# Hymba encoder layer on one core: the output projection by Strassen's seven products, all local heads in the second token chunk, low weight parts kept in DRAM

## The chip, the core and the metric

The kernel runs on one core of a Trainium2 chip. The metric is the device time of one execution in microseconds; lower is better. TensorE (PE in the profile, PEld for its weight loads), VectorE (DVE), ScalarE (ACT) and GpSimd (POOL) compute; SyncE (SP) issues every DMA of this kernel, in the order of its own instruction stream.

## The reference

One encoder layer, applied to a prompt of 1024 tokens and to a sample of 256 tokens, each with 16 meta tokens ahead. All in float32.

```python
def encoder_layer(h, ...):                           # h: tokens x 2048
    u = rms_norm(h, norm_w) @ w_in                   # 2048 x 6656: qa ka va za qb kb vb zb
    qa, ka = axial rope of per-head rms_norm(qa), rms_norm(ka)      # 8 query heads, 2 key heads
    ya = global_gqa(qa, ka, va) * silu(za)           # full attention, 8 heads of 128
    qb, kb = per-head rms_norm(qb), rms_norm(kb)     # 8 heads of 128
    yb = neighbourhood_attention(qb, kb, vb, rpb) * silu(zb)        # 8 x 16 window on a grid 64 wide
    return h + concatenate([ya, yb]) @ w_out         # 2048 x 2048; meta tokens are dropped at the end
```

## The kernel before

Every matrix of the layer is cut in strips of 128 output features, and everything is kept transposed (features on the partitions, tokens along the free axis). A float32 product is done in three matmuls on a rounded high part and a low part: high x high, high x low, low x high. `split` makes the two parts: ScalarE rounds the high part (L54), VectorE subtracts it from the full value (L55). So every tile of weights (`wr`, 128 x 512, 256 KB) costs one DMA, one ScalarE and one VectorE instruction, and gives `wh` and `wl`.

The 1296 token rows don't fit at once. **Chunk 1** (L431) has the meta tokens, the sample and 384 prompt tokens, **chunk 2** (L539) the other 640 prompt tokens. Each loads its x, splits it (L85, L86), and runs the 52 strips of the input projection (`strips`, L108: per strip 4 weight tiles, and 16 x 2 x 3 matmuls, L128 to L130). Both chunks read and split all the weights. Chunk 1 also does the sample's attention. Chunk 2 does the prompt's: 8 global heads of 4 blocks (`attend`, L243), with strips between them, and then the local heads (`attend_strip`, L338), 4 blocks each. Strips of the last four local heads (`NL = 4`) are done ahead, two after each global head (`FILL_A`), their results put in DRAM (`k2d`, `q2d`, `vn`, `zd`); their attention (`late_blocks`) is left for the output projection.

An attention block is a chain: score matmuls (L254 to L256, or L359 to L361), a maximum over partitions on GpSimd (L202), subtraction and exponential, a sum over partitions on GpSimd (L219), the matmuls with v (L294 to L296, or L393), and `put_y`, which scales, multiplies by z, splits the result into two parts and stores both in DRAM (`yd`).

The **output projection** (`outproj`, L758) is done in two halves of the 2048 inputs, eight heads each: the first half's y (`yh`, both parts, 1280 tokens, 1.25 MB a head) is loaded, 16 strips of 72 matmuls run (blocks of 512, 512 and 256 tokens), the sum with x goes to DRAM (`pd`), and the 16 blocks of the last four local heads are put between the first 12 strips. The second half does the same with the other heads and adds `pd`.

The order on each engine is made by a scheduler that works on a simulated timeline of the program, by priority and by what is ready; `high_priority(offset=woff)` moves weight loads and splits ahead. An engine, and SP, executes its stream in order. Buffers per tile name are the pools' `bufs` (4 for `raw`, 4 for `w`, 1 for `q`, `k`, `v`, `z`).

Of the kernel before, what the change touches and what calls it, by code (L numbers as in the profile page):

```python
# [37 lines left out]
NL = 4  # L38
FILL_A = 2
FILL_B = 1  # L40
LSTR = 12
YORD = (0, 4, 1, 5, 2, 6, 3, 7)
WCH = 4
OBL = [(0, 512), (512, 512), (1024, 256)]
# [3 lines left out]
class Kern:  # L48
# [59 lines left out]
    def strips(self, jobs, getx):  # L108

        nc, tc = self.nc, self.tc  # L110
        out = [[pool.tile([P, 512], F32, tag=tag, name="pp") for pool, tag in pools] for _, _, pools in jobs]
        for c in range(KT // WCH):
            ws = []
            for src, _, _ in jobs:
                with tc.high_priority(offset=self.woff):
                    w = self.raw.tile([P, WCH, P], F32, tag="raw", name="wr")
                    self.lastw = nc.sync.dma_start(w[:], src[:, c * WCH:(c + 1) * WCH, :]).ins
# [104 lines left out]
    def put_y(self, po, tot, zs, ydst):  # L222
# [7 lines left out]
        y = self.t.tile([P, QB], F32, tag="t", name="y")  # L230
# [6 lines left out]
        yt = self.y.tile([P, 2, QB], F32R, tag="y", name="yt")  # L237
        self.split(yt[:, 0, :], yt[:, 1, :], y[:])
        for i, d in enumerate(ydst):
            yi = yt[:, i, :].bitcast(F32)  # L240
            nc.sync.dma_start(d, yi.rearrange("p (g r) -> p g r", g=4) if len(d.shape) == 3 else yi)
# [183 lines left out]
    def project(self, *parts):  # L425

        jobs = [(self.io["w_in"][p[0]], p[1], [p[3] if len(p) > 3 else (self.pp, "pp")] * len(p[1])) for p in parts]
        out = self.strips(jobs, self.get_x)
        return [p[2](ps) for p, ps in zip(parts, out)]

    def chunk1(self):  # L431
        nc, io = self.nc, self.io
        self.woff = 0
# [68 lines left out]
        def run(h, q, z, k, v, vm, tab):  # L502
            k, km = k
            ydst = [self.yd[h][:, i, NP:] for i in range(2)]
# [34 lines left out]
    def chunk2(self):  # L539
        nc, io = self.nc, self.io  # L540
        self.start_chunk(io["x2"], T2)
# [119 lines left out]
        def run_block(h, b, q, z, k, v, tab):  # L661
            k, km = k
            v, vm = v
            if tab is not None:
                c = slice(64 * b, 64 * b + 64)
                self.attend_strip(q, strips_of(z[:])[:, :, c], k, km, v[b], vm[:], tab, b,
                                  [strips_of(self.yd[h][:, i, :NP])[:, :, c] for i in range(2)])
# [3 lines left out]
            self.attend(q[:, :, c], z[:, c], keys, km, v, vm[:], [self.yd[h][:, i, c] for i in range(2)])  # L671
# [5 lines left out]
        def late_blocks():  # L677
            for h in range(NH - NL, NH):
# [9 lines left out]
        for h in range(NH - NL, NH):  # L688
# [3 lines left out]
        late = late[:-2] + [late[-2:]]  # L692

        def fill(n):
            for _ in range(min(n, len(late))):
                p = late.pop(0)
                pr(*(p if isinstance(p, list) else [p]))

        for g in range(2):
# [5 lines left out]
            for h in range(4 * g, 4 * g + 4):  # L705
# [3 lines left out]
                fill(FILL_A)  # L709
        for h in range(NH - NL):  # L710
            for what in "kqvz":
                if what == "z":
                    z, = pr(z_strip(ZB + h, 8 + h))
                elif what == "v":
                    pr(v_local(VB + h, h))
                    v = v_windows(h)
                elif what == "q":
                    q, = pr(q_strip(QB_ + h, 8 + h, qwb, False))
                else:
                    k, = pr(k_strip(KB + h, 2 + h, kwb, False))  # L720
            run(8 + h, q, z, k, v, self.bias_table(h))
            fill(FILL_B if h < NH - NL - 1 else len(late))
        self.late_blocks = late_blocks()


    def load_y(self, pool, heads):
        nc = self.nc
        for h in heads:
            y = pool.tile([P, 2, NP + NS], F32R, tag=f"y{h}", name="yh")
            nc.sync.dma_start(y[:].bitcast(F32), self.yd[h][:])  # L730
            self.ys[h] = y[:, 0, :], y[:, 1, :]

    def out_strip(self, c, half, third):

        nc, tc = self.nc, self.tc
        ps = [self.pp.tile([P, 512], F32, tag="pp", name="pp") for _ in range(2)]
        ps.append(third[0].tile([P, 512], F32, tag=third[1], name="pp"))
        ws = []
        for i in range(2 * half, 2 * half + 2):
            with tc.high_priority(offset=self.woff):  # L740
                w = self.raw.tile([P, WCH, P], F32, tag="raw", name="wr")
                self.lastw = nc.sync.dma_start(w[:], self.io["w_out"][c][:, i * WCH:(i + 1) * WCH, :]).ins
                wh = self.w.tile([P, WCH, P], F32R, tag="wh", name="wh")
                wl = self.w.tile([P, WCH, P], F32R, tag="wl", name="wl")
                self.split(wh[:], wl[:], w[:])
                ws += [(wh[:, k, :], wl[:, k, :]) for k in range(WCH)]
        order = range(8) if half else YORD
        for blocks in (OBL[:2], OBL[2:]):
            for i, k in enumerate(order):
                wh, wl = ws[k]  # L750
                yh, yl = self.ys[8 * half + k]
                for o, n in blocks:
                    p = ps[o // 512]
                    nc.tensor.matmul(p[:, :n], wh, yh[:, o:o + n], start=i == 0, stop=False)  # L754
                    nc.tensor.matmul(p[:, :n], wh, yl[:, o:o + n], start=False, stop=False)  # L755
                    nc.tensor.matmul(p[:, :n], wl, yh[:, o:o + n], start=False, stop=i == 7)  # L756
        return ps

    def outproj(self, es_attn):

        nc, io = self.nc, self.io
        NT = NP + NS
        self.ys = {}
        self.load_y(self.ya, YORD)
        done = 0
        for c in range(16):
            while done < 4 * NL and done * LSTR < 4 * NL * (c + 1):
# [134 lines left out]
```

## Time and profile before

| | |
|---|---|
| three runs | 2297.64, 2296.99, 2293.76 us; median 2296.99 |
| the profiled execution | 2295.91 us, span 2294.1 us, granted clock 0.999 |
| instructions | 40464 |
| busy | PE 2268.6, PEld 2192.9, DVE 1601.9, ACT 1104.6, POOL 530.9 us |
| DMA | 290.17 MB, mean 126 GB/s |

A matmul row's duration counts from its start to the end of its results; the next matmul starts long before that end. So "busy" says whether PE had something running, and the cost of a matmul is the distance from its start to the next one's start. DVE and ACT rows overlap a little in the same way. DMA share is that of 16 engines.

### The profile page before, as it was taken

Reading aid. Unit: us, or ns where it says so; the run is one execution under the profiler, and the core shown is the slowest. Engines: PE = TensorE matmul, PEld = TensorE weight load, DVE = VectorE, ACT = ScalarE, POOL = GpSimd, SP = SyncE. Lnnn points to the kernel's source line nnn. Section 1 sums busy time; section 2 is a strip of 40 time slices with the busy share of each in tenths; the row PEclk is TensorE's granted clock in tenths of the full one; section 3 lists DMA queues with packets and bytes.
Section 4 is the critical chain, followed back from the end, with each engine's and each line's share of the span. In section 5 each row is a group of like instructions: output and inputs, shape, how many; then the busy total and the mean of one; then the engine's idle time right before and its main releaser. Section 6 shows DMA issues by size and latency. Waiting matters only on the chain.

```text
span 2294.1 us, 40464 instructions
## 1 busy us (share of the span) xinstructions
PE 2268.6 (99%) x15166; PEld 2192.9 (96%) x15166; DVE 1601.9 (70%) x3092; ACT 1104.6 (48%) x2400; POOL 530.9 (23%) x275
## 2 busy tenths in 40 slices
PE   7999999999999999999999999999999999999999
PEld 7999999999999999999999999999999888888888
DVE  6876775555555689999998989998777666652221
ACT  6654554444444566676666665665454333320000
POOL 0322232211121124223223314223233222210000
PEclk9999999999999999999999999999999999999999
DMA  6433333333333442222222222224444966657342
GB/s 199 137 111 112 110 105 111 107 106 106 102 108 107 134 153 72 90 86 75 91 93 87 88 81 75 87 84 138 116 133 115 336 214 191 191 182 277 133 136 79
DMA packets 205733, 290.17 MB, mean 126 GB/s; under 512 B 55360, under 2 KB 125408, under 8 KB 203488
## 3 DMA queue, kind: packets, MB, share of 16 engines
q1 hardware_dynamic: 205536, 287.58, 39.5%
q8 instruction: 119, 1.95, 0.4%
q14 instruction: 78, 0.64, 0.1%
HBM read 216.30 MB, written 64.63 MB: 122 GB/s over the span
## 4 chain that ended last, share of the span: by engine, by line
PE 54%; DVE 3%; ACT 1%; POOL 1%; issue 1%; DMA 1%; SPq 0%; DVEq 0%; POOLq 0%
PE pp L130 8%; PE pp L129 8%; PE pp L128 8%; PE pp L754 7%; PE pp L755 7%; PE pp L756 7%; PE po L393 2%; PE po L296 1%; PE po L294 1%; PE po L295 1%; PE sp L254 1%; PE sp L255 1%; PE sp L256 1%; POOL m L138 1%; PE sp L361 1%
## 5 line engine op out<-in xcount | busy, mean ns | idle before, releaser
L128 PE MATMUL pp<-xh,wh 128*128 128x384 f32 (+2 forms) x3328 | 1025.2, 311 | 11.8 <-ACT xh L85 11.6
L129 PE MATMUL pp<-xl,wh 128*128 128x384 f32 (+2 forms) x3328 | 1030.7, 310 | 1.1 <-DVE xl L86 0.8
L130 PE MATMUL pp<-xh,wl 128*128 128x384 f32 (+2 forms) x3328 | 1029.8, 311 | 0.0
L128 PEld LDWEIGHTS pp<-xh,wh 128*128 128x128 f32 x3328 | 624.1, 188 | 13.7 <-ACT xh L85 13.1
L129 PEld LDWEIGHTS pp<-xl,wh 128*128 128x128 f32 x3328 | 625.8, 188 | 3.4 <-DVE xl L86 3.3
L130 PEld LDWEIGHTS pp<-xh,wl 128*128 128x128 f32 x3328 | 625.7, 188 | 0.2
L55 DVE TENSOR_TENSOR wl<-wr,wh 128x512 fp32r<-128x512 f32 x480 | 368.7, 771 | 226.1 <-ACT wh L54 220.8
L54 ACT CAST wh<-wr 128x512 fp32r<-128x512 f32 x480 | 294.7, 617 | 416.2 <-PE pp L129 198.3
L138 POOL PARTITION_ALL_REDUCE m<-ms x104 | 246.4, 2369 | 423.2 <-ACT ms L136 299.9
L754 PE MATMUL pp<-yh,wh 128*128 128x512 f32 (+1 forms) x768 | 274.6, 358 | 2.5 <-DMA yh<-yd 2.5
L755 PE MATMUL pp<-yh,wh 128*128 128x512 f32 (+1 forms) x768 | 275.0, 358 | 0.0
L219 POOL PARTITION_ALL_REDUCE tot<-a x80 | 170.3, 2128 | 450.6 <-DVE a L217 450.5
L756 PE MATMUL pp<-yh,wl 128*128 128x512 f32 (+1 forms) x768 | 274.2, 358 | 0.0
L202 POOL PARTITION_ALL_REDUCE ma<-m x80 | 106.9, 1336 | 583.9 <-DVE m L200 570.2
L754 PEld LDWEIGHTS pp<-yh,wh 128*128 128x128 f32 x768 | 145.7, 190 | 24.0 <-DMA yh<-yd 2.6
L755 PEld LDWEIGHTS pp<-yh,wh 128*128 128x128 f32 x768 | 145.7, 190 | 20.9
L756 PEld LDWEIGHTS pp<-yh,wl 128*128 128x128 f32 x768 | 145.5, 190 | 20.8
L785 DVE TENSOR_TENSOR o<-pp,o 128x512 f32<-128x512 f32 (+1 forms) x48 | 28.5, 602 | 140.3 <-PE pp L756 140.3
L258 ACT COPY S<-sp 128x512 f32<-128x512 f32 x136 | 77.7, 581 | 61.1 <-PE sp L256 37.1
L275 ACT ACTIVATE S<-S 128x512 f32<-128x512 f32 x136 | 84.4, 629 | 30.1 <-DVE S L274 30.0
L61 ACT ACTIVATE rs_l<-m 128x384 f32<-128x384 f32 (+2 forms) x104 | 49.1, 472 | 102.4 <-DVE m L139 102.2
L55 DVE TENSOR_TENSOR pl<-S,ph 128x512 fp32r<-128x512 f32 x136 | 96.0, 719 | 0.0
(186 smaller groups left out, 3235.6 us busy)
## 6 DMA issues: line engine op xcount, KB each, us to landing
wr<-in_w_in SPq DMA_DIRECT2D x416, 256.0 KB, 3.2
yd<-yt SPq DMA_DIRECT2D x160, 128.0 KB, 2.4
yh<-yd SPq DMA_DIRECT2D x16, 1280.0 KB, 17.4
wr<-in_w_out SPq DMA_DIRECT2D x64, 256.0 KB, 4.0
pd<-o SPq DMA_DIRECT2D x16, 640.0 KB, 4.3
o<-pd SPq DMA_DIRECT2D x16, 640.0 KB, 5.0
bt<-in_bt SPq DMA_DIRECT2D x16, 576.0 KB, 5.3
vw<-vn SPq DMA_DIRECT2D x32, 256.0 KB, 3.6
```

The lines of the kernel that those rows point to most:

```text
L54: nc.scalar.copy(hi, full)
L55: nc.vector.tensor_tensor(out=lo, in0=full, in1=hi.bitcast(F32), op=ALU.subtract)
L128: nc.tensor.matmul(p[:, :n], wh[:, k, :], xh[:, o:o + n], start=first, stop=False)
L129: nc.tensor.matmul(p[:, :n], wh[:, k, :], xl[:, o:o + n], start=False, stop=False)
L130: nc.tensor.matmul(p[:, :n], wl[:, k, :], xh[:, o:o + n], start=False, stop=last)
L138: nc.gpsimd.partition_all_reduce(m2[:], ms[:], P, RED.add)
L202: nc.gpsimd.partition_all_reduce(ma[:], m1[:], P, RED.max)
L219: nc.gpsimd.partition_all_reduce(tot[:], a1[:], P, RED.add)
L275: nc.scalar.activation(s, s, AF.Exp, scale=SCALE)
L754: nc.tensor.matmul(p[:, :n], wh, yh[:, o:o + n], start=i == 0, stop=False)
L755: nc.tensor.matmul(p[:, :n], wh, yl[:, o:o + n], start=False, stop=False)
L756: nc.tensor.matmul(p[:, :n], wl, yh[:, o:o + n], start=False, stop=i == 7)
```

## The change

1. **Output projection.** y is 2048 features x 1280 tokens, w_out 2048 x 2048. Both are cut in halves, and the four block products of 8 strips x 8 heads x 640 tokens are replaced by seven products (`order = (1, 2, 5, 6, 7, 3, 4)`) of sums and differences of blocks. One product is 8 strips of 48 matmuls, each on 320 tokens (L851 to L853 of the new file). VectorE makes the sums of the y blocks (`y_operand`), of the weight blocks (`w_operand`; two of them kept in DRAM as `td` for a later product) and of the results (`out_sums`). y is stored once, unsplit, and split when it is loaded.
2. **Local heads.** All eight heads' strips are done as `late` ones, one after each global head, and the remaining 24 after them with 28 attention blocks between; the four blocks of the last head run between the first strips of product 1.
3. **Low weight parts.** Chunk 1 stores each `wl` to DRAM (`wld`, 52 x 1 MB); chunk 2 loads it instead of computing it, so that L55 on weights goes away there.

```diff
-                    self.split(wh[:], wl[:], w[:])
-                    ws.append((wh, wl))
+                    if self.second:
+                        nc.sync.dma_start(wl[:].bitcast(F32), self.wld[s][:, c * WCH:(c + 1) * WCH, :])
+                        nc.scalar.copy(wh[:], w[:])
+                    else:
+                        self.split(wh[:], wl[:], w[:])
+                ws.append((wh, wl))
+                if not self.second:
+                    nc.sync.dma_start(self.wld[s][:, c * WCH:(c + 1) * WCH, :], wl[:].bitcast(F32))
...
-        yt = self.y.tile([P, 2, QB], F32R, tag="y", name="yt")
-        self.split(yt[:, 0, :], yt[:, 1, :], y[:])
...
+        nc.sync.dma_start(ydst, y[:].rearrange("p (g r) -> p g r", g=4) if len(ydst.shape) == 3 else y[:])
...
-                fill(FILL_A)
-        for h in range(NH - NL):
...
+                fill(FILL)
+        self.blocks = local_blocks()
+        n, done = len(late), 0
+        for i in range(n):
+            fill(1)
+            while done < 4 * (NH - 1) and done * n < 4 * (NH - 1) * (i + 1):
+                next(self.blocks)
+                done += 1
...
+    def y_operand(self, p, k):
+        nc = self.nc
+        if p in (1, 2):
+            v = self.y_half(8 * (p - 1) + k, 0)
+        elif p == 4:
+            v = self.y_half(8 + k, 1)
+        elif p == 7:
+            v, b = self.y_half(k, 0), self.y_half(k, 1)
+            nc.vector.tensor_tensor(out=v, in0=v, in1=b, op=ALU.subtract)
...
+        t = self.ym.tile([P, 2, TH], F32R, tag="ym", name="ym")
+        self.split(t[:, 0, :], t[:, 1, :], v)
+        return t
...
+    def w_operand(self, p, s):
...
+                    x, y = {5: ((w[8 + s], i), (w[s], i)), 6: ((w[8 + s], 8 + i), (self.td[s][0], i)),
+                            7: ((w[8 + s], 8 + i), (w[8 + s], i)), 4: ((self.td[s][1], i), (w[s], 8 + i))}[p]
+                    v, b = load(*x), load(*y)
+                    nc.vector.tensor_tensor(out=v, in0=v, in1=b, op=ALU.subtract)
+                    if p in (5, 6):
+                        nc.sync.dma_start(self.td[s][p - 5][:, i:i + WCH, :], v)
...
+                self.split(wh[:], wl[:], v)
...
+    def out_sums(self, p, s, ps):
...
+        else:
+            c, half = {7: (8 + s, 1), 3: (8 + s, 0), 4: (s, 1)}[p]
+            src = self.U[s] if p == 4 else self.V[s]
+            o = self.ob.tile([P, TH], F32, tag="o", name="o")
+            self.x_half(o, c, half)
+            add(o[:], o[:], src[:])
+            if p == 4:
+                add(two(o), two(o), ps, ALU.subtract)
+            else:
+                add(two(o), ps, two(o))
+            if p == 7:
+                add(two(self.U[s]), ps, two(self.U[s]))
+            self.store(o, c, half)
...
+        for n, p in enumerate(order):
+            nxt = []
+            for s in range(8):
+                ws = self.w_operand(p, s)
+                ps = self.pq.tile([P, 2, 512], F32, tag="pq", name="pq")
+                for k in range(8):
+                    wh, wl = ws[k]
+                    yh, yl = ys[k][:, 0, :], ys[k][:, 1, :]
+                    for b in range(2):
+                        o = slice(B * b, B * b + B)
+                        nc.tensor.matmul(ps[:, b, :B], wh, yh[:, o], start=k == 0, stop=False)
+                        nc.tensor.matmul(ps[:, b, :B], wh, yl[:, o], start=False, stop=False)
+                        nc.tensor.matmul(ps[:, b, :B], wl, yh[:, o], start=False, stop=k == 7)
+                self.out_sums(p, s, ps)
+                if n == 0:
+                    next(self.blocks, None)
+                if n < 6 and (n or s > 3):
+                    for _ in range(1 if n else 2):
+                        nxt.append(self.y_operand(order[n + 1], len(nxt)))
...
-                                   ("t", 6), ("y", 1)):
+                                   ("t", 6), ("y", 2)):
...
+                for name, bufs in (("yr", 4), ("ym", 10), ("us", 8), ("ob", 2)):
+                    pool(es_y, name, bufs, side="right", **kw)
+                def end_attention():
+                    es_attn.close()
+                    for name, bufs in (("ysp", 1), ("w", 6), ("raw", 8)):
+                        pool(es_y, name, bufs, side="right", **kw)
```

The change moves instructions on every engine. Three places are shown.

The first is SP's stream in the middle of chunk 1, where local heads' strips run; `qd`, `vmd`, `vn` and `zd` are results on their way to DRAM. Before:

```order
L117 DMA wr_4832<-in_w_in 128x512
L474 DMA vmd2_89<-vm_4389 16x128 x3
L117 DMA wr_4898<-in_w_in 128x512
L413 DMA vm3_255<-vmd2_89 48x128
L117 DMA wr_4928<-in_w_in 128x512
```

After:

```order
L114 DMA wr_6299<-in_w_in 128x512
L124 DMA wld46_217<-wl_6100 128x512
L473 DMA vmd4_91<-vm_5849 16x128 x3
L114 DMA wr_6366<-in_w_in 128x512
L124 DMA wld31_202<-wl_6209 128x512
L412 DMA vm3_307<-vmd4_91 48x128
L114 DMA wr_6397<-in_w_in 128x512
```

Behind each weight load now stands a store of a low part. At the very start of the program the same happens: the load of the second x tile, which stood ahead of every wait, now stands behind the first such store.

The second is SP's stream in chunk 2 among the global heads, where tiles of the next heads are loaded (`kf`, `q`) and results go out (`yd`) or are swapped between partitions (`ts`). Before:

```order
L241 DMA yd3_174<-yt_13777 128x256 x2
L145 DMA ts_14477<-t_14475 32x256 x4
L117 DMA wr_14783<-in_w_in 128x512
L117 DMA wr_14813<-in_w_in 128x512
L117 DMA wr_14843<-in_w_in 128x512
L551 DMA kf_14319<-kd1_68 128x2x400
L117 DMA wr_14873<-in_w_in 128x512
```

After:

```order
L601 DMA q_13058<-qd3_100 128x2x384
L118 DMA wl_13877<-wld9_180 128x512
L114 DMA wr_14051<-in_w_in 128x512
L148 DMA ts_13214<-t_13212 32x256
L240 DMA yd2_157<-y_12650 128x256
L148 DMA ts_13214<-t_13212 32x256 x3
L118 DMA wl_13907<-wld9_180 128x512
L114 DMA wr_14081<-in_w_in 128x512
```

The loads of `wl` stand between those of `wr`; a `wl` load waits until PE is through with the `wl` tile four tiles back, while the `wr` loads behind it are for tiles further on.

The third is PE's stream at the start of the output projection. Before, the last score matmuls of an earlier head (`sp`) are followed by the projection's (`pp`), which need `yh`:

```order
L360 MATMUL sp_22368<-q_21799,kf_21643 128x192
L361 MATMUL sp_22368<-q_21799,kf_21643 128x192
L754 MATMUL pp_22668<-yh_22501,wh_22673 128x512
L755 MATMUL pp_22668<-yh_22501,wh_22673 128x512
L756 MATMUL pp_22668<-yh_22501,wl_22674 128x512
```

After, 33 matmuls of product 1 (`pq`, on split y tiles `ym`) stand between the last score matmul of the seventh local head and the first one of the eighth, whose `q` and `kf` are loaded into the only buffer after the seventh's last use; these are the last two of the 33 and what follows them:

```order
L852 MATMUL pq_23504<-ym_23311,wh_23494 128x320
L853 MATMUL pq_23504<-ym_23311,wl_23495 128x320
L358 MATMUL sp_23434<-q_23427,kf_23411 128x128
L359 MATMUL sp_23434<-q_23427,kf_23411 128x128
L389 MATMUL po_23269<-Pm_306,vm3_307 128x256
L392 MATMUL po_23269<-S_23228,vw_22606 128x128 x2
L392 MATMUL po_23269<-S_23229,vw_22606 128x192 x2
L851 MATMUL pq_23356<-ym_23326,wh_23352 128x320
```

So the last head's scores, which stood deep inside the first half of the projection, now stand within its first strip.

More of the change, by code (lines that the diff above doesn't have):

```diff
@@ L425, in project @@
     def project(self, *parts):
-        jobs = [(self.io["w_in"][p[0]], p[1], [p[3] if len(p) > 3 else (self.pp, "pp")] * len(p[1])) for p in parts]
+        jobs = [(p[0], p[1], [p[3] if len(p) > 3 else (self.pp, "pp")] * len(p[1])) for p in parts]
         out = self.strips(jobs, self.get_x)
@@ L432, in chunk1 @@
         nc, io = self.nc, self.io
-        self.woff = 0
+        self.woff, self.second = 0, False
         self.start_chunk(io["x1"], T1)
@@ L503, in run @@
             k, km = k
-            ydst = [self.yd[h][:, i, NP:] for i in range(2)]
+            ydst = self.yd[h][:, NP:]
             if tab is not None:
@@ L540, in chunk2 @@
         nc, io = self.nc, self.io
+        self.second = True
         self.start_chunk(io["x2"], T2)
@@ L675, in run, with local_blocks @@
                 run_block(h, b, q, z, k, v, tab)
-        def late_blocks():
-            for h in range(NH - NL, NH):
+        def local_blocks():
+            for h in range(NH):
                 k, v = k_load(2 + h), v_windows(h)
@@ L723, in chunk2 @@
[L723 to L742, printed above, removed]
+                fill(FILL)
@@ new lines, in w_operand, with load @@
+    def w_operand(self, p, s):
+        nc, tc = self.nc, self.tc
+        ws = []
+        def load(src, i):
+            r = self.raw.tile([P, WCH, P], F32, tag="raw", name="wr")
+            nc.sync.dma_start(r[:], src[:, i:i + WCH, :])
+            return r[:]
+        for i in range(0, 8, WCH):
+            with tc.high_priority(offset=self.woff):
+                w = self.io["w_out"]
+                if p in (1, 2):
+                    v = load(w[s], 8 * (p - 1) + i)
+                elif p == 3:
+                    v = load(w[8 + s], 8 + i)
+                else:
+                    x, y = {5: ((w[8 + s], i), (w[s], i)), 6: ((w[8 + s], 8 + i), (self.td[s][0], i)),
[4 more added lines that the diff above has]
+                        nc.sync.dma_start(self.td[s][p - 5][:, i:i + WCH, :], v)
@@ new lines, in outproj @@
+    def outproj(self, end_attention):
+        nc = self.nc
+        B = TH // 2
+        self.U, self.V = {}, {}
+        order = (1, 2, 5, 6, 7, 3, 4)
+        ys = [self.y_operand(1, k) for k in range(8)]
+        for n, p in enumerate(order):
[17 more added lines that the diff above has]
+                        nxt.append(self.y_operand(order[n + 1], len(nxt)))
+            if n == 0:
+                for _ in self.blocks:
+                    pass
+                end_attention()
+            ys = nxt
@@ L828, in build @@
                 es_x.close()
-                pool(self.es_y, "ya", 1, side="right", reuse_waits="tile")
-                pool(self.es_y, "ob", 3, side="right", reuse_waits="tile")
-                self.outproj(es_attn)
+                es_pp.close()
+                kw = {"reuse_waits": "tile"}
+                pool(es_y, "pq", 2, space=PSUM, **kw)
+                for name, bufs in (("yr", 4), ("ym", 10), ("us", 8), ("ob", 2)):
[4 more added lines that the diff above has]
+                        pool(es_y, name, bufs, side="right", **kw)
+                    self.ysum = [self.ysp.tile([P, TH], F32, tag=f"ys{k}", name="ysum") for k in range(8)]
+                self.outproj(end_attention)
 def _grid(rows):
```

139 lines of the change are left out of this document (66 added, 73 removed).

## The prediction

> **What bounds the kernel now.** I read the page's busy times first, then a table by stage, then single matmul rows, then what PE and SP wait for.
>
> ```profile
> span 2294.1 us, 40464 instructions
> PE 2268.6 (99%) x15166; PEld 2192.9 (96%) x15166; DVE 1601.9 (70%) x3092; ACT 1104.6 (48%) x2400; POOL 530.9 (23%) x275
> ```
>
> PE has something running in all but 25 us. The stages show where those are (columns: stage, length, then PE, PEld, DVE, ACT, POOL busy with counts, granted clock, DMA share, GB/s):
>
> ```profile
> 0.00:50.00 50.00, 38.28 (x228) 35.21 (x229) 32.54 (x42) 31.89 (x47) 2.07 (x10) 1.00 0.66 204
> 50.00:800.00 750.00, 750.00 (x5156) 749.65 (x5155) 468.18 (x863) 355.21 (x779) 167.34 (x83) 1.00 0.36 112
> 800.00:850.00 50.00, 48.70 (x332) 47.71 (x331) 42.83 (x70) 33.82 (x70) 13.52 (x5) 1.00 0.55 172
> 850.00:1570.00 720.00, 714.53 (x5175) 710.00 (x5174) 667.08 (x1265) 471.21 (x1024) 219.07 (x102) 1.00 0.27 86
> 1570.00:1780.00 210.00, 210.00 (x1491) 209.82 (x1491) 158.20 (x343) 103.26 (x242) 69.24 (x37) 1.00 0.44 125
> 1780.00:1800.00 20.00, 16.73 (x93) 14.52 (x92) 9.01 (x22) 7.02 (x18) 3.36 (x2) 0.83 1.01 382
> 1800.00:2050.00 250.00, 250.00 (x1442) 218.79 (x1442) 169.38 (x400) 82.17 (x190) 56.29 (x38) 1.00 0.66 207
> 2060.00:2080.00 20.00, 20.00 (x106) 17.06 (x105) 3.01 (x5) 1.14 (x2) 0.00 (x0) 1.00 1.01 429
> 2080.00:2280.00 200.00, 200.00 (x1046) 172.42 (x1045) 45.79 (x73) 17.39 (x28) 0.00 (x0) 1.00 0.43 143
> ```
>
> Chunk 1 ends near 800, the global heads run from 850 to 1570, the directly computed local heads to 1780, then the output projection. Only the first 50 us (11.7 us idle), the global stage (5.5) and the hand-over at 1780 to 1800 (3.3, and the clock falls) lose PE time. DVE is at 93% in the global stage and nowhere else close. So PE's own work sets the time, and the change is worth what it takes from PE, less new waits.
>
> **Term 1, the output projection's matmuls.** The cost is the distance between starts:
>
> ```profile
> 300.51 0.28 PE L128 MATMUL pp<-xh,wh 128*128 128x256 f32 x1
> 300.86 0.34 PE L128 MATMUL pp<-xh,wh 128*128 128x384 f32 x1
> 301.39 0.28 PE L128 MATMUL pp<-xh,wh 128*128 128x256 f32 x1
> ...
> 2152.44 0.40 PE L754 MATMUL pp<-yh,wh 128*128 128x512 f32 x1
> 2153.83 0.39 PE L754 MATMUL pp<-yh,wh 128*128 128x512 f32 x1
> ...
> L754 PE MATMUL pp<-yh,wh 128*128 128x512 f32 (+1 forms) x768 | 274.6, 358 | 2.5 <-DMA yh<-yd 2.5
> ```
>
> Three of 256 take 0.35 us (0.117 each), three of 384 take 0.53 (0.177), six of 512 take 1.39 (0.232). The six of the first pattern average 320 columns: 0.88 / 6 = 0.1467 us, my price for a 320-column matmul, which no row shows. Before there are three groups of 768 like the one shown, 2304, two of 512 to one of 256: by these rows (2 x 0.232 + 0.117) / 3 = 0.193, by the stage 2080:2280 200 / 1046 = 0.191; I take 0.1923, 443 us. After there are 7 x 8 x 48 = 2688, 394 us. Strassen's 7/8 in columns is thus 49 us of PE time, between 46 and 51 by the two prices. The other matmuls stay as they are.
>
> **Term 2, the hand-over.** Before, PE waits 2.5 us for `yh`, then runs slowly:
>
> ```profile
> 1790.08 0.80 PE L754 MATMUL pp<-yh,wh 128*128 128x512 f32 x1 [2.46 <-DMA yh<-yd]
> 1790.67 0.63 PE L755 MATMUL pp<-yh,wh 128*128 128x512 f32 x1
> 1791.10 0.63 PE L756 MATMUL pp<-yh,wl 128*128 128x512 f32 x1
> ...
> 1962.98 0.28 PE L361 MATMUL sp<-q,kf 128*128 128x192 f32 x1
> ...
> 1972.29 0.22 PE L359 MATMUL sp<-q,kf 128*128 128x128 f32 x1
> ```
>
> Starts 0.43 us apart instead of 0.232: half the clock, and 0.83 granted over 20 us is 3.4 us lost; 5.9 us in all. After, there is no big `yh` load, but the last local head now starts here. Its reload (k, q from DRAM, split in place) took 9.3 us from one head's last score to the next one's first (1962.98 to 1972.29), under 33 matmuls of 0.147, that is 4.8 us: 4.5 short, with 3.4 for the clock again and 1 for y tiles whose loads queue behind this head's: 8.9, so +3 (bounds -6, if the reload is quicker, and +8). The Trainium skill (TensorE: Matmul & The Clock Gate, part 1) says that idle of about 3.4 us halves the clock; here 2.46 us, after smaller gaps, was enough. By that rule the two later hand-overs of term 6 would also cost 1.7 us each, +3.4 in the sum.
>
> **Term 3, the start.** SP and ACT rows:
>
> ```profile
> 2.10 1.38 SPq L117 DMA_DIRECT2D wr<-in_w_in  x3
> 3.52 1.21 SPq L81 DMA_DIRECT2D xr<-in_x  x2
> ...
> 5.47 0.62 ACT L54 CAST wh<-wr 128x512 fp32r<-128x512 f32 x1 [3.48 <-DMA wr<-in_w_in]
> ...
> wr<-in_w_in SPq DMA_DIRECT2D x416, 256.0 KB, 3.2
> wr<-in_w_out SPq DMA_DIRECT2D x64, 256.0 KB, 4.0
> ```
>
> The second x tile, issued at 3.5, now waits behind the store of the first `wl`, ready near 6.8 (wh at 6.1, then one DVE subtraction): 3.3 us later, in a stage that already waits for x. +3, bounds 0 and +8.
>
> **The rest of both chunks.** Chunk 1 gets 208 stores of 256 KB, 54.5 MB in some 800 us, 68 GB/s on top of 112 at a share of 0.36: share about 0.58, cover enough. SP issues one in 0.46 us (1.38 for three); 8 weight DMAs take 3.7 us of a strip's 14.1 (96 x 0.1467). It costs nothing; if SP blocks, four tiles of weights (14 us) are the cover, and without them every strip would wait. Chunk 2's start has x and weights at 172 GB/s; +1 there (0 to 4).
>
> **Term 4, the global heads.** Removed per block: four `wl` splits; one of four strips; the split of y. DVE prices:
>
> ```profile
> L55 DVE TENSOR_TENSOR wl<-wr,wh 128x512 fp32r<-128x512 f32 x480 | 368.7, 771 | 226.1 <-ACT wh L54 220.8 <-DMA ts<-t 1.8 <-PE sp L256 0.7
> L55 DVE TENSOR_TENSOR yt<-y,yt 128x256 fp32r<-128x256 f32 x80 | 38.0, 475 | 9.3 <-ACT yt L54 8.4 <-DMA wr<-in_w_in 0.5
> 1360.18 2.49 DVE L274 TENSOR_TENSOR S<-S,ma 128x512 f32<-128x512 f32 x4
> ```
>
> Per block PE had 714.5 / 32 = 22.3 us and DVE 20.8, with one strip to fill in. After, three quarters of a strip stand there: PE loses 3.5 us (a quarter of 14.1), DVE the 4 splits of 0.62 (four in 2.49) to 0.77 and the y split's 0.48, 17.3 to 17.9 left, and some evacuation work that I don't count. That is 92 to 95% of 18.8, where it was 93%. There is less filler, but DVE is shorter in proportion, so the chain of a block is too: 0, bounds -2 and +8. The low parts now come by DMA: a `wl` load waits for PE to release the buffer four tiles back, so it has three tiles, 10.6 us, against 3.2 to land.
>
> **Term 5, the local heads.** The meta scores of each block tell how fast the blocks followed each other in the output projection:
>
> ```profile
> L190 PE MATMUL sp<-q,km x17: 278/280/284, 1801.1 to 2013.5; 128*48 128x256 f32 x17
> ```
>
> Sixteen steps in 212.4 us, 13.3 us each, with four reloads among them and no idle PE (1800:2050). After, 24 strips carry 28 blocks: 24 / 28 x 14.1 us plus some 3 us of the block's own matmuls (12 scores 0.11 apart, four of 256 columns, four with v) make 15 us a block, more cover than the 13.3 that sufficed. But now every head is reloaded, and what was hidden by long strips of 512 columns may show once or twice: +2, bounds 0 and +12 (a fourth of eight reloads of 9.3 uncovered is 19, which I leave to the rivals).
>
> **Term 6, inside the seven products.** One product is 384 x 0.1467 = 56.3 us, 7.04 a strip. The busiest for DVE is product 7: per strip two weight differences and two splits (4 x 0.62), y difference and split (2 x 0.78, that is 0.62 x 640/512), and three sums of 640 (2.4): 6.4 of 7.04, tight, elsewhere 2.8 to 5.6. DMA in product 6 is 48 tiles of 256 KB (w_out, and `td` both ways) and 16 halves of y of 320 KB, 17.8 MB or 316 GB/s; products 5 and 7 have 15.2 and 16.3 MB, 270 and 289 GB/s. The trace has 382 and 429 at a share of 1.01. So both fit, barely: +2.5 (0 to 15). Product 1 ends with the last head's four blocks, whose y product 2 needs, and product 7's operands take two loads each through four buffers that come free late: +3 for the two hand-overs (0 to 10). The last evacuation is 640 wide instead of 256: +0.5.
>
> **Sum.** 2295.9 (the profiled execution; the median of the runs is 1.1 higher) - 49 + 3 + 3 + 1 + 0 + 2 + 2.5 + 3 + 0.5 = 2261.9. I forecast 2262.
>
> **Rivals.**
> - *All waits hidden*: term 1 at its upper price of 51, hand-over no worse, others at nothing: 2245 to 2252. For it: PE idles nowhere between 50 and 800 or 1570 and 1780. Against: the start and the reload are worked out from rows.
> - *Attention comes late in chunk 2*: with less filler PE waits at each of the 32 global blocks. The longest such waits of the stage are 1 to 1.4 us (L294 1.4, L254 1.1):
>
> ```profile
> PE po L294 <- ACT ph L54: 1.4, 1, 1.4
> PE sp L254 <- ACT Sm L194: 1.1, 1, 1.1
> ```
>
>   At 0.8 a block that is +25: 2287. Against it: the DVE ratio of term 4.
> - *DMA gives out in products 5 to 7*, the case on the other side. They need 49.3 MB in 169 us, 292 GB/s. At 222, near the 207 of the stage 1800:2050, they take 222 us, +53: 2315. It decides below about 243 GB/s, where it costs the 34 us that the sum leaves. For it: loads, stores and waits for DVE share one queue in order, and `yh` loads made the share 1.01. Against: 207 was demand at a share of 0.66.
> - *A 320-column matmul costs as one of 384*, since a fixed part per matmul, not the columns, sets the distance: 2688 x 0.177 = 476, +33 instead of -49: 2344. It decides from (443 - 15) / 2688 = 0.159 on, with the 15 us of the other terms. Against: 0.117, 0.177, 0.232 lie almost on a line. The Trainium skill (the same page, Back-to-back issue gap) has a rule of that kind: a stream spaced at about 81 ns for 128 columns and 131 for 512. By a line through these, an estimate from that page, 2304 cost 276 us and 2688 cost 285, a loss of 9. The trace disagrees: 0.117 at 256 and 0.232 at 512.
> - *No change*: waits eat just the gain.
>
> **Chances.** Forecast (2252 to 2275) 0.62; all hidden 0.10; late attention (2275 to 2291) 0.14; no change 0.03; DMA 0.08; flat matmuls 0.03. A measurement of this kernel tells no less than 0.2%, 4.6 us. Faster 0.86, same 0.03, slower 0.11. The range 2244 to 2288 takes in the first three but the last 3 us.
>
> **What would show it.** Right: matmul starts 0.147 apart in `pq`, 56 to 58 us a product; idle in the first 50 us grown to 14 or 15; a wait of 3 to 6 us at the last head's first scores with a dip of the clock; DVE about 90% in the global stage; DMA near 300 GB/s in product 6. Wrong: `pq` starts 0.16 or more apart; PE waiting at L254 or L293 over the whole global stage; landings of weight loads of 10 us and more, and PE waiting for `wh` in products 5 to 7.

## The result, and the profile after

The changed kernel takes 2313.2 us (median, 2311.6 to 2314.9) against 2296.1 for the kernel before: ratio 1.0076, 95% interval 1.0058 to 1.0093. It is slower by 17 us where 34 us of gain were forecast, and outside the range. The execution profiled here took 2312.79 us.

First the page's span, busy times and the matmul groups of the new output projection (last columns: idle time ahead of the group, and what ended most of it), then the group of the weight differences and the loads of w_out:

```profile
span 2311.0 us, 42251 instructions
PE 2239.2 (97%) x15550; PEld 2223.9 (96%) x15550; DVE 1599.8 (69%) x2988; ACT 1152.3 (50%) x2432; POOL 511.5 (22%) x275
...
L851 PE MATMUL pq<-ym,wh 128*128 128x320 f32 x896 | 283.8, 318 | 29.6 <-DVE u L804 13.0
L852 PE MATMUL pq<-ym,wh 128*128 128x320 f32 x896 | 284.3, 318 | 15.9 <-DVE ym L51 15.9
L853 PE MATMUL pq<-ym,wl 128*128 128x320 f32 x896 | 282.3, 316 | 0.0
...
L767 DVE TENSOR_TENSOR wr<-wr 128x512 f32<-128x512 f32 x64 | 44.2, 691 | 104.3 <-DMA wr<-in_w_out 73.9
...
wr<-in_w_out SPq DMA_DIRECT2D x144, 256.0 KB, 4.4
```

PE is busy 29 us less than before, but in a span 17 us longer: 72 us have no matmul, where it was 25. And VectorE's weight differences sat 104 us waiting, nearly all for weight loads. The stages (columns as before; the rows from 1837 on are products 1, 2, 5, 6, 7, 3, 4 in that order):

```profile
0.00:50.00 50.00, 35.94 (x190) 32.75 (x191) 30.72 (x39) 29.94 (x42) 1.32 (x9) 0.97 0.75 229
800.00:850.00 50.00, 45.69 (x305) 44.93 (x305) 31.09 (x50) 33.06 (x63) 9.94 (x4) 0.97 0.77 248
850.00:1500.00 650.00, 649.66 (x4780) 648.72 (x4779) 576.88 (x1122) 446.73 (x968) 205.40 (x105) 1.00 0.46 136
1500.00:1837.00 337.00, 329.77 (x2345) 328.18 (x2343) 225.50 (x514) 167.24 (x382) 114.48 (x66) 1.00 0.70 206
1837.00:1909.00 72.00, 71.85 (x491) 71.85 (x492) 58.76 (x117) 37.98 (x76) 13.86 (x9) 0.96 0.68 219
1909.00:1965.00 56.00, 56.00 (x384) 56.00 (x383) 32.37 (x47) 17.31 (x27) 0.00 (x0) 1.00 0.94 317
1965.00:2024.00 59.00, 57.66 (x390) 56.87 (x389) 31.32 (x47) 19.98 (x33) 0.00 (x0) 1.00 0.83 256
2024.00:2098.00 74.00, 61.78 (x383) 60.39 (x381) 40.80 (x60) 13.23 (x22) 0.00 (x0) 0.91 0.59 179
2098.00:2173.00 75.00, 61.43 (x384) 59.06 (x384) 45.84 (x66) 18.95 (x30) 0.00 (x0) 0.95 0.69 211
2173.00:2241.00 68.00, 59.39 (x385) 58.09 (x386) 35.50 (x52) 12.37 (x20) 0.00 (x0) 0.97 0.62 184
2241.00:2311.00 70.00, 60.48 (x384) 58.62 (x383) 29.84 (x43) 8.08 (x13) 0.00 (x0) 0.95 0.44 140
```

Product 2 runs 384 matmuls in 56.0 us with no idle time, at 317 GB/s. Products 6, 7, 3 and 4 have the same 384 matmuls in 68 to 75 us at 140 to 211 GB/s, with VectorE busy at most 61% of the time. Neither DMA nor VectorE is full there. In these four rows PE has no matmul in 12.2 + 13.6 + 8.6 + 9.5 = 44 us (5 of them are the end after the last matmul), and 243 us of matmuls stand where 4 x 56.3 = 225 would do: 18 us of slow clock behind the gaps.

For the stage accounts below I take PE's loss: for each matmul the distance to the next one's start, less the median of its shape (0.147 us for 320 columns), summed by stage where it is over 25 ns. It contains idle time and slow clock.

| PE's loss, us | before | after | difference | forecast |
|---|---|---|---|---|
| first 50 us | 8.7 | 14.0 | +5.3 | +3 |
| start of chunk 2 (800 to 850) | 2.6 | 6.9 | +4.3 | +1 |
| global heads (850 to 1570 before, to 1500 after) | 11.1 | 2.8 | -8.3 | 0 |
| local heads, the hand-over, and what is left of them in the output projection | 16.0 | 20.8 | +4.8 | +5 |
| products 2, 5, 6, 7, 3, 4 | - | 59.1 | +59.1 | +5.5 |
| rest of chunk 1 | 3.1 | 4.2 | +1.1 | 0 |

The sum is +66.3. With -51 for the matmuls (2688 x 0.1467 = 394.3 against 1536 x 0.2303 + 768 x 0.1191 = 445.2, the mean distances where nothing is lost) and +1.4 for the end it gives +16.7; the spans differ by 16.9. So nearly the whole error lies in one row.

What stands there is seen best at the beginning of product 6, on four engines: a ScalarE row, then VectorE, SyncE's DMA issues, and PE (brackets: the idle time ahead and what ended it):

```profile
2017.78 1.48 ACT L50 CAST ym<-ysum 128x640 fp32r<-128x640 f32 x2
...
2021.37 0.69 DVE L767 TENSOR_TENSOR wr<-wr 128x512 f32<-128x512 f32 x1 [5.41 <-DMA wr<-td]
2021.98 0.68 DVE L51 TENSOR_TENSOR wl<-wr,wh 128x512 fp32r<-128x512 f32 x1
2025.41 0.69 DVE L767 TENSOR_TENSOR wr<-wr 128x512 f32<-128x512 f32 x1 [2.75 <-DMA wr<-td]
2026.02 0.69 DVE L51 TENSOR_TENSOR wl<-wr,wh 128x512 fp32r<-128x512 f32 x1
2030.23 0.69 DVE L767 TENSOR_TENSOR wr<-wr 128x512 f32<-128x512 f32 x1 [3.52 <-DMA wr<-td]
2030.84 0.68 DVE L51 TENSOR_TENSOR wl<-wr,wh 128x512 fp32r<-128x512 f32 x1
2031.44 0.82 DVE L51 TENSOR_TENSOR ym<-ysum,ym 128x640 fp32r<-128x640 f32 x1
...
2022.09 0.32 SPq L753 DMA_DIRECT2D wr<-td  x1
2022.46 0.42 SPq L769 DMA_DIRECT2D td<-wr  x1
2022.94 0.42 SPq L753 DMA_DIRECT2D wr<-in_w_out  x1
2026.13 0.32 SPq L769 DMA_DIRECT2D td<-wr  x1
2026.55 0.38 SPq L753 DMA_DIRECT2D wr<-td  x1
2027.02 0.41 SPq L753 DMA_DIRECT2D wr<-in_w_out  x1
...
2025.37 0.31 PE L851 MATMUL pq<-ym,wh 128*128 128x320 f32 x1
2032.32 0.63 PE L852 MATMUL pq<-ym,wh 128*128 128x320 f32 x1 [6.63 <-DVE ym L51]
2032.75 0.47 PE L853 MATMUL pq<-ym,wl 128*128 128x320 f32 x1
2033.01 0.47 PE L851 MATMUL pq<-ym,wh 128*128 128x320 f32 x1
```

PE needs `ym`, whose VectorE split (0.82 us at 2031.44) has all it needs long before: ScalarE rounded this y tile at 2017.78 (the first of the two in that row), and the sum is older. It stands in VectorE's stream behind weight differences of strips that PE reaches 31 to 35 us later, and each of these waits 2.8 to 5.4 us for a load. The loads come late for a reason of their own: SyncE goes on when VectorE has finished a difference. The load of 2022.09 follows the difference of 2021.37, which gives back one of its two raw buffers; the loads of 2026.55 and 2027.02 stand behind the store of the difference of 2025.41. A load lands 3 to 4 us later, and VectorE is already standing at the difference that needs it. So VectorE goes round with one landing per turn, and PSUM evacuations and y splits wait in line. In the page's words this is "DVE wr L767 <- DMA"; for PE it shows as "<- DVE", since PE sees only its own neighbour. From product 5 to the end these waits come to:

```profile
DVE wr L767 <- DMA wr<-in_w_out: 63.9, 31, 5.2
DVE o L804 <- DMA o<-in_x: 48.8, 16, 6.8
DVE wr L767 <- DMA wr<-td: 26.7, 12, 5.4
```

The Trainium skill (PSUM — Partial Sum Buffer, Engine vs sequencer instructions) says that VectorE's queue is strict first in, first out. The rows above agree: a split that was ready at about 2018.6 began at 2031.44, behind three differences that waited for loads.

Not every wait of PE lies under a landing. The longest of product 7 is for an evacuation,

```profile
2126.08 0.49 PE L851 MATMUL pq<-ym,wh 128*128 128x320 f32 x1 [5.15 <-DVE u L804]
```

and VectorE works without a pause from 2117.43 on: y sums for the next product and splits stand ahead of the evacuation. That is the order of its stream too, but VectorE waits for no load while PE waits.

### The profile page after: what moved, and what is told of

Read it like the earlier page. It is cut to its first block, busy times and chain, and to the rows that moved or that the text cites. A ratio compares the mean times of both kernels' runs of the same rounds, so it can differ in the third digit from the quotient of the medians.

```text
span 2311.0 us, 42251 instructions
## 1 busy us (share of the span) xinstructions
PE 2239.2 (97%) x15550; PEld 2223.9 (96%) x15550; DVE 1599.8 (69%) x2988; ACT 1152.3 (50%) x2432; POOL 511.5 (22%) x275
## 3 DMA queue, kind: packets, MB, share of 16 engines
q1 hardware_dynamic: 275040, 413.44, 58.5%
## 5 line engine op out<-in xcount | busy, mean ns | idle before, releaser
L131 PE MATMUL pp<-xh,wh 128*128 128x384 f32 (+2 forms) x3328 | 1027.6, 312 | 16.9 <-ACT xh L81 16.9
L50 ACT CAST wh<-wr 128x512 fp32r<-128x512 f32 x320 | 198.0, 619 | 426.5 <-PE pq L852 213.1
L51 DVE TENSOR_TENSOR wl<-wr,wh 128x512 fp32r<-128x512 f32 x320 | 246.6, 774 | 187.9 <-ACT wh L50 147.1
L141 POOL PARTITION_ALL_REDUCE m<-ms x104 | 233.8, 2248 | 410.8 <-ACT ms L139 332.5
L851 PE MATMUL pq<-ym,wh 128*128 128x320 f32 x896 | 283.8, 318 | 29.6 <-DVE u L804 13.0
L852 PE MATMUL pq<-ym,wh 128*128 128x320 f32 x896 | 284.3, 318 | 15.9 <-DVE ym L51 15.9
L853 PE MATMUL pq<-ym,wl 128*128 128x320 f32 x896 | 282.3, 316 | 0.0
L222 POOL PARTITION_ALL_REDUCE tot<-a x80 | 164.5, 2056 | 438.0 <-DVE a L220 435.7
L851 PEld LDWEIGHTS pq<-ym,wh 128*128 128x128 f32 x896 | 173.2, 194 | 33.6 <-issue 17.6
L852 PEld LDWEIGHTS pq<-ym,wh 128*128 128x128 f32 x896 | 173.7, 194 | 19.5 <-DVE ym L51 19.5
L853 PEld LDWEIGHTS pq<-ym,wl 128*128 128x128 f32 x896 | 173.7, 194 | 0.0
L119 ACT CAST wh<-wr 128x512 fp32r<-128x512 f32 x208 | 127.7, 615 | 56.7 <-PE pp L132 49.1
L767 DVE TENSOR_TENSOR wr<-wr 128x512 f32<-128x512 f32 x64 | 44.2, 691 | 104.3 <-DMA wr<-in_w_out 73.9
L51 DVE TENSOR_TENSOR pl<-S,ph 128x512 fp32r<-128x512 f32 x136 | 101.5, 753 | 7.3 <-ACT ph L50 7.0
```

Source lines behind the costliest of these rows:

```text
L50: nc.scalar.copy(hi, full)
L51: nc.vector.tensor_tensor(out=lo, in0=full, in1=hi.bitcast(F32), op=ALU.subtract)
L119: nc.scalar.copy(wh[:], w[:])
L131: nc.tensor.matmul(p[:, :n], wh[:, k, :], xh[:, o:o + n], start=first, stop=False)
L141: nc.gpsimd.partition_all_reduce(m2[:], ms[:], P, RED.add)
L222: nc.gpsimd.partition_all_reduce(tot[:], a1[:], P, RED.add)
```

## The experiments

Each is an edit of the changed kernel, and its ratio is to the kernel before, run beside it. The in-order theory is the one just told; the rivals are bandwidth, PSUM tiles and SyncE's queue.

**SyncE's queue** (`gq`). Stores of differences and results, and the x loads, are issued by GpSimd.

```diff
-                        nc.sync.dma_start(self.td[s][p - 5][:, i:i + WCH, :], v)
+                        nc.gpsimd.dma_start(self.td[s][p - 5][:, i:i + WCH, :], v)
```
(and so in `x_half` and `store`)

> The changed kernel took 2313 us; its products 6, 7, 3 and 4 last 75, 75, 67 and 65 us where the matmuls alone need 56, and PE waits there for VectorE, which waits for DMA. Here the stores of td and of the results and the loads of x are issued by GpSimd, which has nothing else to do then, so that SyncE's stream holds loads of weights and of y alone. Theory 1 (a loop through in-order queues: a store that waits for VectorE stands ahead of the next loads on SyncE, and VectorE waits for those loads with PSUM evacuations behind): the four products fall by 20 us or more in sum, to 2293 or less. Theory 2 (the DMA engines can't move more): the same bytes move, so within 5 us of 2313. Theory 3 (two PSUM buffers are too few): within 5 us of 2313.

2312.0 us, 1.0076 (1.0057 to 1.0095), as the changed kernel. In the total this is what the two rivals gave. Loss in products 6, 7, 3 and 4 falls from 57 to 38 us, but products 1 and 2 lose 16 where it was 4. VectorE's waits for weight loads from product 5 on stay: 67.1 + 22.3 = 89 us (changed kernel 90.6). So the shared queue is a part of it and not the cause. Why products 1 and 2 got worse was not tried.

**Deeper buffers** (`deep`). 12 raw tiles instead of 8, 4 output tiles instead of 2.

> Twelve weight tiles in flight instead of eight (raw) and four output tiles instead of two (ob) in the products; nothing else. Theory 1 (in-order queues): more loads may be issued before a store stands in the way, and x loads no longer wait for the store two strips back: 10 to 25 us less than 2313, most of it in products 6, 7, 3, 4. Theory 2 (DMA engines are full): no gain, within 5 us. Theory 3 (PSUM): within 5 us.

2295.7 us, 1.0003 (0.9991 to 1.0014): 17.5 us better, with 63 us of waits for weight loads and 36 us of loss in the four products. More tiles in flight shorten each wait (longest 3.2 us instead of 5.4) and don't remove it.

**More PSUM** (`psum4`). The attention's PSUM pools are closed when attention ends, and every second strip from product 2 on uses a second pair of tiles.

```diff
-                ps = self.pq.tile([P, 2, 512], F32, tag="pq", name="pq")
+                ps = (self.pq2 if n and s % 2 else self.pq).tile([P, 2, 512], F32, tag="pq", name="pq")
```

> After the attention has ended, its four PSUM banks serve as two more buffers for the products' sums, so that PE may run four strips ahead of VectorE's evacuation instead of two. Theory 3 (two PSUM buffers are too few): the waits of the first matmul of a strip for VectorE's sums (21 us in all) go, 2290 to 2298. Theory 1 (in-order queues): a part of these waits only moves to the waits for y parts and weights, since VectorE itself is late: 2303 to 2313. Theory 2 (DMA engines are full): no more than 5 us.

2304.6 us, 1.0035 (1.0025 to 1.0045). Weight waits 90 us, as in the changed kernel, but PE loses 10 us less in the four products. From product 5 on PE no longer waits for evacuations here, yet waits longer for `ym` (15.9 us in the changed kernel):

```profile
PE pq L852 <- DVE ym L51: 35.7, 9, 9.1
```

**Part 3 undone** (`no_wld`). Chunk 2 splits its weights on VectorE again; nothing is stored.

> Undoes one part of the change: no low weight part goes to DRAM, chunk 2 splits its weights on VectorE as chunk 1 does. Theory: the stores at the two chunk starts cost about 10 us (PE is 38.3 us busy in the first 50 us before, 35.9 after, and 48.7 against 45.7 in 800 to 850), and these come back; in exchange VectorE gets 208 x 0.6 to 0.77 us more in chunk 2, which shows as waits of PE only in the global stage. Rival: VectorE, with one strip less of cover per global head, then becomes the bound in the global stage (17.3 + 1.9 of splits against 18.8 us of PE per block, over 100%): 20 to 40 us slower than 2313. By the first 2300 to 2306.

2326.9 us, 1.0139 (1.0123 to 1.0155), between the two forecasts: part 3 is worth 13.7 us here. Its costs are seen (without it the loss at the start is 9.6 instead of 14.0, at chunk 2's start 0.8 instead of 6.9), and so is what it buys in the global heads, where PE was busy 649.7 of 650 us with it:

```profile
850.00:1500.00 650.00, 631.54 (x4542) 625.99 (x4541) 605.76 (x1137) 426.10 (x910) 206.17 (x93) 0.98 0.26 75
```

**VectorE's order** (`behind3`). The test of the in-order theory: the same instructions, buffers and loads, but a strip's differences and splits stand on VectorE behind the evacuation of the strip three before. (`after(BACK)`, with `BACK = 3`, ties VectorE's instructions of the block to the last one of that evacuation by order alone.)

```diff
-                    nc.vector.tensor_tensor(out=v, in0=v, in1=b, op=ALU.subtract)
+                    with self.after(BACK):
+                        nc.vector.tensor_tensor(out=v, in0=v, in1=b, op=ALU.subtract)
...
-                self.split(wh[:], wl[:], v)
+                with self.after(BACK):
+                    self.split(wh[:], wl[:], v)
```

> Only VectorE's order changes: the weight differences and the splits of a strip of the output projection are put on VectorE behind the PSUM evacuation of the strip three before it (in the changed kernel they stand up to six strips ahead). Loads, buffers and PSUM stay as they are. Theory 1 (VectorE executes in order, and differences placed far too early in its stream wait 3 to 5 us for their loads with the evacuations and splits queued behind them): the matmuls' idle time in products 6, 7, 3 and 4, 57 us in the changed kernel, falls to under 30, and the time comes to 2280 to 2290 us. Theory 2 (the loads themselves come too slowly: bandwidth, or the round from a released buffer to the next landing): the differences wait as long as before and now come later, so 2313 us or more. Theory 3 (too few PSUM tiles): evacuations are no later than before at the same depth, 2305 to 2313 us.

2276.1 us, 0.9923 (0.9908 to 0.9938): 37 us from the order of instructions, 4 more than the best forecast, and the kernel is faster than before the change. The waits for weight loads fall from 90.6 to 14.9 us:

```profile
DVE o L810 <- DMA o<-in_x: 55.8, 15, 7.4
...
DVE wr L772 <- DMA wr<-in_w_out: 8.3, 5, 3.1
...
DVE wr L772 <- DMA wr<-td: 6.6, 6, 1.4
```

Loss in products 6, 7, 3 and 4 is 20 us, in product 6 none. Bandwidth falls as a cause: same bytes, same buffers, later differences, less time.

Two things about the edit are less simple than its description. It doesn't reach every strip: product 5 is evacuated by ScalarE, so its strips don't count, and its last seven strips and the first three of product 6 stand behind evacuations of product 2, farther back than three. That splits the 32 strips with differences into two groups. In the 22 that are tied, VectorE's waits for weight loads, summed over the strips' own differences, fall from 73.1 us to 0.0; in the ten others from 27.5 to 17.0. And the scheduler, which makes all streams, moved other instructions too: about a third of SyncE's 389 issues in the products stand elsewhere. But this didn't bring the loads sooner. Those of products 6 and 7 were issued 28 and 25 us (means) before the strip that uses them began, where it was 38 and 44; and the waits for x grew from 48.8 to 55.8 us. So the waits went because VectorE came later, not because the data came earlier.

**The y sums too** (`behind3y`). The differences and splits in `y_operand` stand behind the evacuation two before.

> As the run with weight differences and splits behind the evacuation of the strip three before, and the sums and splits of the attention output for the next product too, behind the evacuation two before. Theory 1: a few us below that run, 2272 to 2288 us, the gain in products 6 and 7, where two loads each feed a sum. Theory 2: 2313 us or more. If the y sums then come too late, products 6, 7 and 3 begin late by 3 us each, which would show as a wait of the first matmul of a product for ym.

2268.4 us, 0.9885 (0.9871 to 0.9900), again 4 us under the forecast. Product 7 falls from 65.8 to 58.5 us, as expected of two loads for each sum. Products 5 and 6 here, one at 333 GB/s with 1 us idle, one with none:

```profile
1965.00:2023.00 58.00, 57.01 (x386) 56.22 (x385) 37.99 (x56) 19.78 (x32) 0.00 (x0) 1.00 0.96 333
2023.00:2080.00 57.00, 57.00 (x391) 57.00 (x390) 37.98 (x55) 12.75 (x21) 0.00 (x0) 1.00 0.69 216
```

**Five and one before** (`behind5`, `behind1`). `behind3` with another distance.

> The weight differences and splits of a strip behind the evacuation of the strip five before; nothing else changed. In-order theory: with eight raw tiles the loads of such a strip can hardly have landed by then, so VectorE waits nearly as in the changed kernel, and the time lies between 2276 us (three before) and 2313 us (up to six before): 2295 to 2313 us. If the gain of the run with three came from something else than the distance (for instance from the order of differences and splits among themselves), 2276 us.

> The weight differences and splits of a strip behind the evacuation of the strip one before, as late as they can stand without standing behind their own need; nothing else changed. In-order theory: landings are no longer waited for at all (under 10 us of waits of VectorE for weight loads), but the weights now come after the strip before has been evacuated, so TensorE waits in every strip for the two differences and splits, some 2 to 3 us each in products 5, 6, 7 and 4 and 1 to 2 us in products 2 and 3: 2330 to 2420 us. If distance does not matter and only the removal of the waits counts, 2276 us or less.

Five: 2292.4 us, 0.9988 (0.9978 to 0.9998), with 39.6 us of weight waits, a little better than the bounds given. One: 2452.9 us, 1.0681 (1.0661 to 1.0702), worse than expected: VectorE waits only 18 us for weight loads from product 5 on, none of it in products 7 and 4, but PE now waits for the weights themselves, up to 6 us at a time:

```profile
PE pq L858 <- ACT wh L51: 76.6, 25, 6.0
```

In the 22 strips that `behind3` ties, the differences began on average 36 us before their strip in the changed kernel, 26 us in `behind5`, 11 in `behind3` (7 to 16) and 1 in `behind1`. So of the three distances the middle one is best: far enough that the split is done when PE comes, near enough that the load has landed when VectorE comes. Two and four were not tried.

**The starts** (`start`). The first two weight strips of each chunk are not kept in DRAM.

```diff
-                if not self.second:
+                if not self.second and s not in NOLD:
```
(`NOLD = (8, 10)`, and the same condition where chunk 2 loads them)

> The first two weight strips of each chunk are not kept in DRAM (no stores at the kernel's start, no loads of low parts at the second chunk's start; VectorE splits them again). If the stores ahead of the x loads cost the start its 5.3 us over before, and the loads of low parts the second chunk's start its 4.3 us, the time falls by 8 to 9 us to 2304 to 2305 us, and the idle matmul time up to 50 us falls from 14.0 to about 9. If the start is bound by the x loads and not by the stores, the time stays at 2313 us.

2297.1 us, 1.0015 (1.0006 to 1.0024), 16 us better. The loss in the first 50 us falls from 14.0 to 10.1 and at chunk 2's start from 6.9 to 2.5, the 8 us expected. The other 8 were not: product 6 lost 12.6 instead of 17.8, and smaller amounts came elsewhere, on code that was not edited and in streams that are almost the same (386 of SyncE's 389 issues in the products, 417 of VectorE's 424 instructions, keep their order). That a waiting loop on VectorE makes the time depend on small shifts far ahead of it would explain this; it was not tested, and the profiled execution (2293.7 us) was the quickest of ten.

**All together** (`best1`): `behind3y`, `deep`, `psum4` and `start`.

> All together: the weight differences, the splits and the y sums behind the evacuations (three and two strips before), 12 raw tiles instead of 8, 4 output tiles instead of 2, a second pair of PSUM tiles once attention has ended, and no low parts kept for the first two strips of a chunk. Theory 1: the idle time in products 6, 7, 3 and 4 falls below 15 us and 8 us come from the starts, so 2255 to 2270 us, faster than both kernels. Theory 2: not below the run with deeper buffers less the starts, 2287 us.

2253.7 us, 0.9826 (0.9810 to 0.9842). Loss in products 6, 7, 3 and 4: 8.2 us, all in the last two, where VectorE waits for x tiles with y splits behind.

**x loads and stores of the last three products on GpSimd** (`best2`), and **product 4's stores back on SyncE** (`best3`, whose edit is shown; in `best2` all these stores are on `nc.gpsimd`).

```diff
-            self.x_half(o, c, half)
+            self.x_half(o, c, half, nc.gpsimd)
...
-            self.store(o, c, half)
+            self.store(o, c, half, nc.sync if p == 4 else nc.gpsimd)
```

> As the run with all together (2253.7 us), and in the last three products the x loads and the output stores are issued by GpSimd instead of SyncE. What is left there is 2.9 us before the second group of matmuls of product 3 and 5.2 us in product 4, each a wait for ym splits that stand on VectorE behind a sum waiting for its x tile (38.5 us of such waits in all). If SyncE's order (an x load behind loads of weights whose tiles are not free yet, or behind a store that waits for VectorE) makes the x tiles late, the waits of VectorE for x fall below 15 us and the time to 2245 to 2249 us. If the x tiles are late for want of output tiles or of DMA bandwidth, it stays at 2254 us.

> As the run with x loads and stores of the last three products issued by GpSimd (2253.6 us), but the stores of product 4, the last, go back to SyncE. There all seven products but the first ran without a wait of TensorE, and the time after the last matmul began grew from 4.5 to 10.6 us. If the last stores are late because GpSimd issues them behind waits of its own, the end falls back to 4.5 us and the time to 2246 to 2249 us. If the end is the landing of the last store itself, 2253 us.

`best2`: 2253.6 us, 0.9821 (0.9805 to 0.9838). The waits for x fell from 38.5 us to 26.7 only, not below 15: GpSimd's x loads wait 66 us for the stores that give their output tiles back. But PE's loss in all products from 2 on went to nothing; the 8 us won there went into an end of 10.6 us instead of 4.5 and scattered losses before. `best3`: 2245.7 us, 0.9790 (0.9776 to 0.9803), the fastest of all, with the end back at 4.6. Its seven products:

```profile
1826.00:1900.00 74.00, 71.52 (x486) 70.33 (x487) 56.16 (x114) 37.55 (x77) 19.33 (x18) 0.97 0.70 219
1900.00:1957.00 57.00, 57.00 (x391) 57.00 (x390) 33.45 (x49) 16.82 (x28) 0.00 (x0) 1.00 0.87 282
1957.00:2013.00 56.00, 56.00 (x384) 56.00 (x383) 35.72 (x52) 20.06 (x32) 0.00 (x0) 1.00 0.95 328
2013.00:2069.00 56.00, 56.00 (x384) 56.00 (x383) 39.20 (x57) 12.63 (x21) 0.00 (x0) 1.00 0.67 212
2069.00:2126.00 57.00, 57.00 (x391) 57.00 (x390) 47.12 (x68) 19.05 (x30) 13.93 (x26) 1.00 0.89 297
2126.00:2182.00 56.00, 56.00 (x384) 56.00 (x383) 30.63 (x45) 12.24 (x20) 14.45 (x27) 1.00 0.65 207
2182.00:2243.00 61.00, 56.61 (x386) 56.34 (x385) 30.30 (x45) 8.61 (x14) 5.86 (x11) 1.00 0.47 152
```

Six of the seven run at PE's own pace. Product 6 does it at 212 GB/s, so its 179 in the changed kernel was a result of the waiting, not its cause. Nor does it need the 316 GB/s of the prediction: 23 of its 32 weight loads are issued during product 5, which has 328.

## Why the prediction was wrong

The step that failed is term 6, inside the seven products: +5.5 forecast, +59 measured. It compared VectorE's work with the length of a strip (6.4 of 7.04 us) and the bytes with a rate seen elsewhere, found that both fit, and took the rest as slack. Both did fit, as `best3` shows. What it left out is the order in which VectorE meets its work: 64 differences were added to the stream, each needing a fresh load, with evacuations and y splits behind them. The prediction checked for added waits on SyncE's queue and at the hand-overs, and never asked what is queued behind a VectorE instruction that waits for a DMA. The rows were there: weight landings of 4.0 us, and VectorE as the engine that frees both the raw buffer and PSUM. The ranges of that step, 0 to 15 inside the products and 0 to 10 for their hand-overs, were too narrow for a wait that can repeat at each of 64 differences.

The rival on the other side (DMA gives out) named almost the right time, 2315 us, by the wrong cause. It takes a low DMA rate in products 5 to 7, and the rate was low (179 to 256 GB/s where they need 292). But the other signs that the prediction gave for it were absent: weight loads landed in 4.4 us (median), not 10, and PE waited 0.6 us for `wh`. And `behind3y` and `best3` move the same bytes with almost no wait in these products.

The other terms:
- Term 1 was right: starts 0.147 us apart, worth 51 us, the upper price. The flat-cost rival fell.
- Term 2 and term 5 together came out at the right size (+4.8 against +5), but not in kind. PE waits 5.3 us ahead of the first `pq` (to 1837.2) for the PSUM evacuation of the last z strip (L179, at 1836.60). k and q of the last head, which the text had in mind, are not what it waits for. The evacuation stands on VectorE behind steps of an attention block and two y splits; VectorE pauses there for only some 0.6 us between 1831.5 and 1836.6. So it is again the order on VectorE, but hardly a wait for a load. No run tested it: `best3` still has it (5.2 us). That the size came out right is luck.
- Term 3: the mechanism is seen (the second x tile is issued at 6.90 us, behind the store of 6.53; before at 3.52), the size was 5.3 instead of 3. The start of chunk 2 cost 4.3 instead of 1.

```profile
2.11 0.43 SPq L77 DMA_DIRECT2D xr<-in_x  x1
2.58 0.91 SPq L114 DMA_DIRECT2D wr<-in_w_in  x2
6.53 0.33 SPq L124 DMA_DIRECT2D wld<-wl  x1
6.90 0.43 SPq L77 DMA_DIRECT2D xr<-in_x  x1
```

- Term 4 gained 8 instead of 0: VectorE is at 89% there (577 of 650), PE at 99.9%. `no_wld` shows that without part 3 the stage loses 31 us, so the rival of late attention was averted by part 3.
- The clock: the waits that the forecast did not have cost twice. After the 6.63 us the matmuls start 0.26 to 0.27 us apart instead of 0.147. Over products 6, 7, 3 and 4 that is the 18 us of slow clock above, a third of the loss. The Trainium skill (TensorE: Matmul & The Clock Gate, part 1) puts the limit at an idle window of about 3.4 us. The trace agrees only roughly: behind a gap of 3.17 us at 2214.8 the granted clock was 0.52, behind one of 2.34 us at 2103 it stayed at 1.00, but gaps of 2.46 us (before the change, 0.50) and 1.94 us (at 2248.2, 0.66) lowered it too. So the length of the gap alone doesn't decide here.

With most of the term's waits taken away (`behind3y`, 2268.4 us) the forecast of 2262 is 6 us off: its products from 2 on still lose 16 us instead of 5.5, the two starts 6 more than forecast, the global heads 8 less, and term 1 gives 2 more.

## What to carry to other kernels

Busy shares and bandwidth say whether work fits; they don't say whether it is met in an order that fits. Where an edit gives an in-order engine instructions that wait for a fresh DMA, list what stands behind each of them, and ask who frees the buffer that the next load needs: if it is the same engine, the wait repeats with every landing. Place such an instruction between the landing and the need, by an explicit order where the scheduler sees no reason for it. Here that was behind the evacuation of the strip three before, 11 us ahead of the need; five before lost 16 us against that, one before 177. And look in the trace at where the instruction came to stand: the order asked for was not in force in ten of the 32 strips.

## What had not been expected of the hardware

Landings of 256 KB loads of w_out took 4.0 us (median) before, 4.4 in the changed kernel and 5.2 in `best2`, whose products ran without a wait: the longer landing did no harm where nobody stood waiting for it. And 317 GB/s (product 2 of the changed kernel) and 328 (product 5 of `best3`) over 56 us did not disturb 384 matmuls at all.
